# A hybrid recurrent decoder step on one core: ten convolution states moved as one contiguous tile instead of strided pieces per unit

## The chip, the core and the metric

The kernel runs on one NeuronCore of a Trainium2 chip. The core has a matrix engine (TensorE, PE in the profile, with its weight loads as PEld), three engines for elementwise work (VectorE or DVE, ScalarE or ACT, GpSimd or POOL), and SyncE (SP), which in this kernel issues every DMA. The engines run side by side, each in the order of its own instruction stream, and wait for each other by semaphores. The metric is device time in microseconds of the whole launch, as a median over runs. Inputs and outputs lie in HBM, tiles in SBUF, results of matmuls in PSUM.

## The reference, cut to what matters

One layer of a decoder is applied to 2048 prompt tokens and to 8 decode sequences of 4 tokens each. Its input projection is split among four head groups A to D; groups A and B put a short causal convolution over time on part of their channels:

```python
def _causal_conv(x, buf, w, b):
    t = x.shape[1]
    xx = jnp.concatenate([buf.astype(x.dtype), x], axis=1)
    y = b + xx[:, 0:t] * w[0]
    for j in range(1, CONV_K):
        y = y + xx[:, j:j + t] * w[j]
    return y, xx[:, t:]
...
    a_qkv, a_conv_new = _causal_conv(a_qkv, a_conv, conv_a_w, conv_a_b)
    aq, ak, av = _split(jax.nn.silu(a_qkv), (QK_A, QK_A, W_A))
    aq = _l2norm(heads(aq, H_A)) * DK_A ** -0.5
...
    b_xbc, b_conv_new = _causal_conv(b_xbc, b_conv, conv_b_w, conv_b_b)
```

`CONV_K` is 4, so the state of a channel is its last 3 inputs. Group A has 768 such channels and B has 512, together ten tiles of 128 channels. For the prompt the old state is zero; for each of the 8 decode sequences it is an input (3 x 8 numbers per channel), and the new states of both are outputs. After the convolution come the recurrences of the four groups ("mixing"), an output projection, a layer norm and a feed-forward layer.

## The kernel before

The prompt is cut into four blocks of 512 tokens (`NB`, `TB`). The 32 decode tokens ride along in the input projection of block 0, which so has 544 columns, and in the feed-forward layer of block 2. The work on TensorE is a sequence of weight units: `do_P` (L1870) goes through the 31 units of `PUNITS` for each block (one unit is 128 output channels of the input projection), `do_W` makes the output projection and `do_F` the feed-forward layer. `gemm` (L671) multiplies one unit: each weight tile comes by a DMA into `wraw`, is split by `w_split` (L642) into a rounded part `whi` (on ACT or DVE) and a rest `wlo` (on POOL or DVE), and three products are added up in PSUM. For 544 columns a unit takes two PSUM tiles of 272, and 48 matmuls.

What comes behind a unit is a generator that does one step and yields: `u_copy`, `u_gate`, `u_conv`, `u_cf` and `u_rows`. The first units of a block are one of rows and four copies; then come the six convolution units of group A, its two gates, the four convolution units of group B, and the others. A finished unit is stored to DRAM (`store_u`, L947, tensors UA to UD, and XA to XD for decode tokens). When all units of a group are stored, that group's chunks can start: `gen_A` (L1326) loads `laA` from UA, transposes it on TensorE, and so on; group A is one stream, the groups B, C and D are another.

All instructions of all engines are put down in one order by a planner that runs while the kernel is being built: `_Sim` keeps a clock for each engine and for the DMA queue, `_Run.tick` (L310) steps each generator once its clock says that its inputs are there. A `dma` (L472) counts in this, too: the end that `_Sim.move` works out for it becomes the time from which the generator may go on. Helpers such as `tvp` and `cpv` choose the engine of an instruction by those clocks. So whatever changes a clock may change the order and the engine of all that follows, but on the chip each engine then runs its stream strictly in order, and SP does so with its DMAs.

`u_conv` (L979) is the function at stake. `halo` is a small tile with the last three columns of the block before; POOL copies it to the front of `r`. In block 0 (`nt > TB`) a tile `rx` (named prx in the profile, 8 sequences x 7 columns, four buffers) takes the three old inputs of each sequence by a DMA (L988), and ACT evacuates the unit's PSUM into `r` and the last four columns of `rx`. After a yield the new states go out: in block 3 the prompt's, three columns of `r` (L1000), and in block 0 the decode sequences', three columns of `rx` (L1002). Then ACT makes the first tap for the prompt columns and, reading `rx`, for the decode columns; DVE adds three more taps for both; `sgm` (L935) makes the SiLU with DVE and ACT in turns. In the first four units of group A, ACT squares the result and TensorE sums it over each head with the constant `bones` (in the profile: pd<-g,con).

At the start, `ln0_start` (L776) loads the tokens, the first weights, the constants and the parameters in a written order, before anything else goes to SP.

Of the kernel before, what the change touches and what calls it, by code (L numbers as in the profile page):

```python
# [10 lines left out]
F32 = mybir.dt.float32  # L11
# [10 lines left out]
NB = 4  # L22
TB = 512
# [334 lines left out]
def _ap(x):  # L358
    return x[:] if callable(x.ap) else x
# [85 lines left out]
def kernel(ctx: ExitStack, tc: tile.TileContext, t):  # L445
# [3 lines left out]
    cst = ctx.enter_context(tc.tile_pool(name="cst", bufs=1))  # L449
# [17 lines left out]
    G = _Eng(R, "pool", nc.gpsimd, _pool_cost)  # L467
# [4 lines left out]
    def dma(out, in_, extra=0.0):  # L472
        nc.sync.dma_start(out=out, in_=in_)
        R.op("dma", R.sim.move(_ap(out), _ap(in_), extra))

    def A(out, in_, func, scale=1.0, bias=0.0):
        S.activation(out=out, in_=in_, func=func, scale=scale, bias=bias)
# [19 lines left out]
    def stt(out, a, s, b, op0, op1):  # L497
        V.scalar_tensor_tensor(out=out, in0=a, scalar=s, in1=b, op0=op0, op1=op1)
# [25 lines left out]
    def g2(dt=F32):  # L524
        return gp.tile([128, NTM], dt, tag="g", name="g")
# [31 lines left out]
    def PR(name, i=0, rows=128):  # L557
        return par[0:rows, PCOL[name] + i:PCOL[name] + i + 1]
# [14 lines left out]
    SD = cst.tile([128, 2, 2, 65], F32, name="SD")  # L573
    for z in (kzA, kzD, SA, SB, SC, SD):
        G.memset(z, 0.0)
    haloA = [cst.tile([128, 3], F32, name=f"haloA{i}") for i in range(6)]
    haloB = [cst.tile([128, 3], F32, name=f"haloB{i}") for i in range(4)]
    for z in haloA + haloB:
        G.memset(z, 0.0)

    epsT = cst.tile([128, 1], F32, name="epsT")
    G.memset(epsT, EPS)
# [43 lines left out]
    def w_get(i):  # L626
        w = sb4.tile([128, 4, 128], F32, tag="wraw", name="wraw")
        dma(w, units[i])
        raws[i] = w
# [146 lines left out]
    def ln0_start():  # L776
# [58 lines left out]
        for k in range(8):  # L835
            half, j = k // 4, k % 4
# [142 lines left out]
    def u_conv(b, ps, nt, g, j):  # L979
        w0 = "cAw" if g == "A" else "cBw"  # L980
        bn = "cAb" if g == "A" else "cBb"
        halo = (haloA if g == "A" else haloB)[j]
        cst_o, cst_s, cs_i = ("pa_conv", "sa_conv", "a_conv_in") if g == "A" else ("pb_conv", "sb_conv", "b_conv_in")
        r = g2()
        G.tensor_copy(r[:, 0:3], halo)
        if nt > TB:
            rx = sb4.tile([128, 8, 7], F32, tag="prx", name="prx")
            dma(rx[:, :, 0:3], t[cs_i][j * 128:j * 128 + 128])  # L988
        for p, a, e in segs(ps, nt):
            if a < TB:  # L990
                e1 = min(e, TB)
                cp(r[:, 3 + a:3 + e1], p[:, 0:e1 - a])
            if e > TB:
                a1 = max(a, TB)
                cp(rx[:, :, 3:7], p[:, a1 - a:e - a].rearrange("p (b t) -> p b t", b=8))
        z = g2()
        yield
        G.tensor_copy(halo, r[:, TB:TB + 3])
        if b == NB - 1:
            dma(t[cst_o][j * 128:j * 128 + 128], r[:, TB:TB + 3])  # L1000
        if nt > TB:
            dma(t[cst_s][j * 128:j * 128 + 128], rx[:, :, 4:7])  # L1002
        w = [PR(w0, j * 4 + k) for k in range(4)]
        A(z[:, 0:TB], r[:, 0:TB], AF.Identity, w[0], PR(bn, j))
        if nt > TB:
            zx = z[:, TB:nt].rearrange("p (b t) -> p b t", b=8)
            A(zx, rx[:, :, 0:4], AF.Identity, w[0], PR(bn, j))
        yield
        for k in range(1, 4):
            stt(z[:, 0:TB], r[:, k:k + TB], w[k], z[:, 0:TB], mult, add)  # L1010
            if nt > TB:
                stt(zx, rx[:, :, k:k + 4], w[k], zx, mult, add)
            yield
        for a in sgm(z, nt):
            yield
        tt(z[:, 0:nt], z[:, 0:nt], a[:, 0:nt], mult, tvp(nt, LATE_U))
        if g == "A" and j < 4:
            yield
            A(a[:, 0:nt], z[:, 0:nt], AF.Square)
            yield  # L1020
            pp = pieces(nt)
            for p, c0, cn in pp:
                mm(p[:, 0:cn], bones, a[:, c0:c0 + cn])
            for p, c0, cn in pp:
                ln(a[:, c0:c0 + cn], p[:, 0:cn], 1.0, epsT)
            ex(a[:, 0:nt], a[:, 0:nt], -0.5)
            yield
            stt(z[:, 0:nt], z[:, 0:nt], 0.125 if j < 2 else 1.0, a[:, 0:nt], mult, mult)
        R.hold(1.0)
        yield  # L1030
        store_u(b, g, j, z, nt)
# [1140 lines left out]

_OUT = {
    "y_prompt": (2048, D), "y_sample": (ND, D),
    "pa_conv": (768, 3), "pa_ssm": (128, 2, 2, 64), "pb_conv": (512, 3), "pb_ssm": (128, 2, 2, 64),
    "pc_ssm": (128, 2, 2, 64), "pd_mem": (128, 2, 2, 65), "pd_mstab": (4, 1),
    "sa_conv": (768, 8, 3), "sa_ssm": (128, 4, 4, 64), "sb_conv": (512, 8, 3), "sb_ssm": (128, 4, 4, 64),
    "sc_ssm": (128, 4, 4, 64), "sd_mem": (128, 4, 4, 65), "sd_mstab": (4, 8),
}
_KP = [0, 2, 1, 3]  # L2180
# [2 lines left out]
def _layout(i):  # L2183
    f = lambda x: np.ascontiguousarray(x, dtype=x.dtype)
    g = {k: np.asarray(v) for k, v in i.items()}
    a = {}
# [3 lines left out]
    z = np.zeros((D, 1), w.dtype)  # L2190
# [38 lines left out]
    m = np.zeros((16, 8), np.float32)  # L2229
    m[8:12] = g["state_d_mstab"][0].T  # L2230
    a["m_init"] = m
    a["a_conv_in"] = f(g["state_a_conv"][0].transpose(2, 0, 1))
    a["b_conv_in"] = f(g["state_b_conv"][0].transpose(2, 0, 1))

    def st(x):
        return f(x.reshape(4, 2, 4, 64, -1).transpose(1, 3, 0, 2, 4).reshape(128, 4, 4, -1))
# [8 lines left out]
def _unlayout(o):  # L2245
    def ps(x):
        y = np.stack([x[64 * h:64 * h + 64, :, h] for h in range(2)])
        return np.ascontiguousarray(y.transpose(2, 0, 1, 3).reshape(1, 1, 4, 64, -1))

    def ss(x):  # L2250
        return np.ascontiguousarray(x.reshape(2, 64, 4, 4, -1).transpose(2, 0, 3, 1, 4).reshape(1, 8, 4, 64, -1))

    inv = _KP
    pd, sd = ps(o["pd_mem"]), ss(o["sd_mem"])
    c = np.ascontiguousarray
    return (
        o["y_prompt"].reshape(1, 2048, D), o["y_sample"].reshape(8, 4, D),
        c(o["pa_conv"].T).reshape(1, 1, 3, 768), ps(o["pa_ssm"]), c(o["pb_conv"].T).reshape(1, 1, 3, 512), c(ps(o["pb_ssm"])[:, :, inv]),
        ps(o["pc_ssm"]), c(pd[..., 0:64]), c(pd[..., 64]), c(o["pd_mstab"].reshape(1, 1, 4)),
        c(o["sa_conv"].transpose(1, 2, 0))[None], ss(o["sa_ssm"]), c(o["sb_conv"].transpose(1, 2, 0))[None], c(ss(o["sb_ssm"])[:, :, inv]),  # L2260
        ss(o["sc_ssm"]), c(sd[..., 0:64]), c(sd[..., 64]), c(o["sd_mstab"].T)[None],
    )

# [17 lines left out]
```

## Time and profile before

| What | us |
|---|---|
| median of three runs | 3034.87 |
| the three runs | 3036.2, 3029.96, 3034.87 |
| profiled execution | 3030.68 |
| span of the profiled execution, first to last instruction | 3028.4 |
| TensorE busy, span | 2873.8 |
| VectorE busy | 2167.6 |
| GpSimd busy | 1592.5 |
| ScalarE busy | 1249.1 |
| mean granted clock of TensorE | 0.985 |

All times in the views are microseconds from the first instruction. L344 stands at nearly every compute instruction and L473 at nearly every DMA, since both go through helpers that record them; so instructions are told apart by their tiles: `g` are the general 128 x 544 tiles, `pd`, `pa__n` and `pb__n` PSUM tiles, `con` the constants, `par` the parameters, `a` and `b` tiles of the mixing streams. A row reads: output tiles <- input tiles, partitions x elements. DMA rows of SP show how long SP was held by issuing, not the landing. In the slices each digit is one fortieth of the span (75.7 us) in tenths; PEclk is the clock that was granted to TensorE, 1.00 being full speed.

### The profile page before, as it was taken

How to read it: one execution, taken by the hardware profiler on the slowest of the kernel's cores; microseconds unless marked ns; L12 is line 12 of the kernel's file. 1: busy time of each engine (PE TensorE's matmuls, PEld its weight loads, DVE VectorE, ACT ScalarE, POOL GpSimd, SP SyncE). 2: the span in 40 equal slices, each digit the busy share in tenths (PEclk: the TensorE clock that was granted, in tenths of full speed). 3: DMA queues.
4: the chain of work that ended last, by engine and by line, in shares of the span. 5: the costliest groups of instructions: out<-in, count | busy, mean ns of one | idle time of the engine just before them, and what ended most of it. 6: DMA issues, size and time to landing. Idle time of an engine off the chain costs nothing. (4 is left out here: it accounts for less than half of the span.)

```text
span 3028.4 us, 48058 instructions
## 1 busy us (share of the span) xinstructions
PE 2873.8 (95%) x16668; PEld 2472.5 (82%) x16668; DVE 2167.6 (72%) x4104; ACT 1249.1 (41%) x2658; POOL 1592.5 (53%) x1958
## 2 busy tenths in 40 slices
PE   7789989999999899999999999999999999999997
PEld 7779778777777778778777777778999999878886
DVE  7677887998897777778776867868664445484455
ACT  4554665574664533333334223333432222432222
POOL 4564845574756445644644465455354454454545
PEclk9899999999999999999999999999999999999999
DMA  5675546456566444445443444455333333333333
GB/s 170 99 183 168 161 132 209 143 159 195 154 174 199 127 124 135 129 132 157 144 141 95 128 133 133 127 149 165 108 105 91 86 117 91 108 114 98 98 95 100
DMA packets 361263, 407.11 MB, mean 134 GB/s; under 512 B 65468, under 2 KB 207804, under 8 KB 361020
## 3 DMA queue, kind: packets, MB, share of 16 engines
q1 hardware_dynamic: 361020, 404.04, 47.0%
q8 instruction: 132, 2.16, 0.3%
q14 instruction: 111, 0.91, 0.1%
HBM read 340.20 MB, written 63.72 MB: 133 GB/s over the span
## 5 line engine op out<-in xcount | busy, mean ns | idle before, releaser
L344 PE MATMUL pd<-g,whi 128*128 128x512 f32 (+2 forms) x8048 | 2224.4, 360 | 7.4 <-DVE g L344 5.5
L344 POOL TENSOR_TENSOR wlo<-wraw,whi 128x512 fp32r<-128x512 f32 x710 | 992.7, 1405 | 1218.5 <-ACT whi L344 1089.9
L344 PEld LDWEIGHTS pd<-g,whi 128*128 128x128 f32 x8048 | 1380.6, 189 | 206.6 <-DVE g L344 9.1
L344 PE MATMUL pd<-g,wlo 128*128 128x512 f32 (+2 forms) x4024 | 1297.7, 353 | 6.0 <-POOL wlo L344 3.7
L344 PEld LDWEIGHTS pd<-g,wlo 128*128 128x128 f32 x4024 | 715.2, 190 | 94.2 <-POOL wlo L344 6.1
L344 ACT ACTIVATE whi<-wraw 128x512 fp32r<-128x512 f32 x813 | 498.8, 626 | 363.0 <-PE pd L344 257.4
L344 DVE TENSOR_TENSOR g<-g 128x512 fp32r<-128x512 f32 (+5 forms) x364 | 357.2, 985 | 177.0 <-ACT g L344 163.5
L344 ACT ACTIVATE g<-pd 128x512 f32<-128x512 f32 (+1 forms) x329 | 167.6, 527 | 512.0 <-PE pd L344 510.5
L344 DVE TENSOR_TENSOR g<-g,pd 128x512 f32<-128x512 f32 (+2 forms) x288 | 159.5, 571 | 220.6 <-PE pd L344 219.9
L344 POOL TENSOR_TENSOR a<-nb,x 128x124 f32<-128x124 f32 (+30 forms) x496 | 199.0, 401 | 101.6 <-DMA nb<-ud32d 71.9
L344 ACT ACTIVATE g<-g 128x512 f32<-128x512 f32 (+5 forms) x334 | 206.5, 635 | 73.6 <-DVE g L344 65.6
L344 POOL TENSOR_TENSOR x<-x,a 128x124 f32<-128x124 f32 (+30 forms) x496 | 208.2, 420 | 38.9
L344 DVE CAST g<-g 128x512 fp32r<-128x512 f32 (+1 forms) x178 | 187.0, 1051 | 10.2 <-POOL g L344 3.2
L344 ACT ACTIVATE b<-b 128x256 f32<-128x256 f32 (+3 forms) x201 | 81.8, 408 | 214.7 <-DVE b L344 206.5
L344 DVE TENSOR_TENSOR wlo<-wraw,whi 128x512 fp32r<-128x512 f32 x122 | 95.9, 787 | 55.9 <-ACT whi L344 55.4
L344 DVE SCALAR_TENSOR_TENSOR g<-g,par 128x512 f32<-128x512 f32 (+1 forms) x128 | 119.3, 942 | 5.0 <-ACT g L344 5.0
L344 DVE TENSOR_TENSOR b<-laC 128x64 f32<-128x64 f32 (+2 forms) x467 | 115.6, 305 | 4.7 <-DMA laC<-UC 4.7
L344 DVE TENSOR_TENSOR kzD<-laC,b 64x128 f32<-64x128 f32 (+1 forms) x228 | 112.1, 492 | 1.7
L344 DVE SCALAR_TENSOR_TENSOR g<-g 128x512 f32<-128x512 f32 (+3 forms) x124 | 99.5, 805 | 18.9 <-ACT g L344 18.5
L344 DVE BATCH_NORM_STATS2 bst<-g 128x6 f32<-128x512 f32 (+1 forms) x98 | 65.9, 685 | 53.3 <-ACT g L344 48.5
L344 POOL TENSOR_TENSOR g<-g 128x512 f32<-128x512 f32 (+3 forms) x54 | 79.8, 1482 | 39.0 <-ACT g L344 39.0
L344 DVE TENSOR_SCALAR g<-g 128x512 int32<-128x512 int32 (+7 forms) x137 | 73.3, 549 | 20.3 <-ACT g L344 19.4
(2600 smaller groups left out, 2813.9 us busy)
## 6 DMA issues: line engine op xcount, KB each, us to landing
wraw<-in_w_dn_u_dram SPq DMA_DIRECT2D x264, 256.0 KB
wraw<-in_w_up_u_dram SPq DMA_DIRECT2D x256, 256.0 KB
wraw<-in_w_in_u_dram SPq DMA_DIRECT2D x248, 256.0 KB
nb<-ud32d SPq DMA_DIRECT2D x128, 256.0 KB
wraw<-in_w_out_u_dram SPq DMA_DIRECT2D x64, 256.0 KB
UC<-g SPq DMA_DIRECT2D x40, 256.0 KB
g<-in_x_prompt_dram SPq DMA_DIRECT2D x32, 256.0 KB
hTd<-g SPq DMA_DIRECT2D x32, 256.0 KB
```

The lines of the kernel that those rows point to most:

```text
L344: r = f(*a, **k)
```

## The change

The ten prompt halos become one tile `halos` of 128 x 10 x 3, cleared by one memset, and the decode states one tile `cvs` of 128 x 10 x 8 x 3. `cvs` is filled by one DMA in `ln0_start`, behind the first four weight tiles; its DRAM tensor has been laid out as the tile is, so that each partition's 240 numbers (960 bytes) lie in one piece on both sides. In `u_conv`, ACT copies a unit's 24 old inputs from `cvs` to `rx` in front of the evacuation, and after the yield copies the 24 new ones back to the same place. The last of the ten units stores the whole `cvs` in block 0, and the whole `halos` in block 3.

```diff
-    haloA = [cst.tile([128, 3], F32, name=f"haloA{i}") for i in range(6)]
-    haloB = [cst.tile([128, 3], F32, name=f"haloB{i}") for i in range(4)]
-    for z in haloA + haloB:
-        G.memset(z, 0.0)
+    halos = cst.tile([128, 10, 3], F32, name="halos")
+    cvs = cst.tile([128, 10, 8, 3], F32, name="cvs")
+    G.memset(halos, 0.0)
...
         w_get(1)
         w_get(3)
+        dma(cvs, t["conv_in"])
...
-        halo = (haloA if g == "A" else haloB)[j]
-        cst_o, cst_s, cs_i = ("pa_conv", "sa_conv", "a_conv_in") if g == "A" else ("pb_conv", "sb_conv", "b_conv_in")
+        halo = halos[:, j if g == "A" else 6 + j]
+        jj = j if g == "A" else 6 + j
         r = g2()
         G.tensor_copy(r[:, 0:3], halo)
         if nt > TB:
             rx = sb4.tile([128, 8, 7], F32, tag="prx", name="prx")
-            dma(rx[:, :, 0:3], t[cs_i][j * 128:j * 128 + 128])
+            cp(rx[:, :, 0:3], cvs[:, jj])
...
         G.tensor_copy(halo, r[:, TB:TB + 3])
-        if b == NB - 1:
-            dma(t[cst_o][j * 128:j * 128 + 128], r[:, TB:TB + 3])
+        if b == NB - 1 and jj == 9:
+            dma(t["p_conv"], halos)
         if nt > TB:
-            dma(t[cst_s][j * 128:j * 128 + 128], rx[:, :, 4:7])
+            cp(cvs[:, jj], rx[:, :, 4:7])
+            if jj == 9:
+                dma(t["s_conv"], cvs)
```

The outputs `p_conv` and `s_conv` are put back into the reference's shapes outside the launch. Three places show how the order moves. First ACT in block 0, around the third convolution unit of group A (its evacuation is the pair of rows before prx<-pd; g<-g of 128x544 are steps of `sgm` and squares of earlier units). Before:

```order
L344 ACTIVATE prx<-pd 128x8x4
L344 ACTIVATE whi<-wraw 128x512
L344 ACTIVATE g<-g 128x544
L344 ACTIVATE g<-g,par 128x512
L344 ACTIVATE g<-prx,par 128x32
L344 ACTIVATE g<-g 128x544 x2
L344 ACTIVATE whi<-wraw 128x512
L344 ACTIVATE g<-g 128x544
L344 ACTIVATE g<-pd,epsT 128x272 x2
```

Now:

```order
L344 ACTIVATE prx<-cvs 128x8x3
L344 ACTIVATE g<-pd 128x272
L344 ACTIVATE g<-pd 128x240
L344 ACTIVATE prx<-pd 128x8x4
L344 ACTIVATE whi<-wraw 128x512
L344 ACTIVATE g<-g 128x544
L344 ACTIVATE cvs<-prx 128x24
L344 ACTIVATE g<-g,par 128x512
L344 ACTIVATE g<-prx,par 128x32
L344 ACTIVATE g<-g 128x544 x2
L344 ACTIVATE whi<-wraw 128x512
L344 ACTIVATE g<-g 128x544
```

The rows are the same but for the two copies, prx<-cvs ahead of the evacuation and cvs<-prx ahead of the taps. Second, SP up to the first load of group A's first chunk, laA<-UA (wraw are weights, UA and XA stores of finished units of group A). Before:

```order
L473 DMA prx<-in_b_conv_in_dram 128x8x3
L473 DMA wraw<-in_w_in_u_dram 128x512
L473 DMA UA_161<-g 128x4x128
L473 DMA XA<-g 128x32
L473 DMA UA_161<-g 128x4x128
L473 DMA XA<-g 128x32
L473 DMA out_sb_conv_dram<-prx 1024x1x3
L473 DMA laA<-UA_161 128x768
```

Now:

```order
L473 DMA wraw<-in_w_in_u_dram 128x512 x2
L473 DMA UA_144<-g 128x4x128
L473 DMA XA<-g 128x32
L473 DMA UA_144<-g 128x4x128
L473 DMA XA<-g 128x32
L473 DMA laA<-UA_144 128x768
```

The strided load and store that stood between the stores of group A and laA are gone. Third, TensorE at the first use of laA (pa__n<-con,laA transposes it; pd<-g,whi and pd<-g,wlo are the weight products of block 0's units). Before:

```order
L344 MATMUL pd<-g,wlo 128x272 x2
L344 MATMUL pd<-g,whi 128x272 x2
L344 MATMUL pa__1954<-con,laA 128x128 x4
L344 MATMUL pd<-g,whi 128x272 x2
L344 MATMUL pd<-g,wlo 128x272 x2
L344 MATMUL pd<-g,whi 128x272 x2
L344 MATMUL pa__1987<-laA,kzA 128x128 x4
```

Now:

```order
L344 MATMUL pd<-g,wlo 128x272 x2
L344 MATMUL pd<-g,whi 128x272 x2
L344 MATMUL pa__1931<-con,laA 128x128 x4
L344 MATMUL pd<-g,whi 128x272 x2
L344 MATMUL pd<-g,wlo 128x272 x2
L344 MATMUL pd<-g,whi 128x272 x2
L344 MATMUL pd<-con,g 128x128 x4
L344 MATMUL pd<-g,whi 128x272 x2
L344 MATMUL pd<-g,wlo 128x272 x2
L344 MATMUL pd<-g,whi 128x272 x2
L344 MATMUL pa__1975<-laA,kzA 128x128 x4
```

Counted in weight products from the program's start, the transposes of laA stand at 786 now and stood at 774, the products of laA and kzA follow after 12 instead of 6, and the fourth of the norm matmuls pd<-g,con stands at 618 where it stood at 654. Further on the two orders differ throughout; TensorE has as many instructions as before. The chunks of group A stand between 63 weight products earlier and 63 later in the first six and 102 to 153 later from the seventh on.

More of the change, by code (lines that the diff above doesn't have):

```diff
@@ L2174 @@
     "y_prompt": (2048, D), "y_sample": (ND, D),
-    "pa_conv": (768, 3), "pa_ssm": (128, 2, 2, 64), "pb_conv": (512, 3), "pb_ssm": (128, 2, 2, 64),
+    "p_conv": (128, 10, 3), "pa_ssm": (128, 2, 2, 64), "pb_ssm": (128, 2, 2, 64),
     "pc_ssm": (128, 2, 2, 64), "pd_mem": (128, 2, 2, 65), "pd_mstab": (4, 1),
-    "sa_conv": (768, 8, 3), "sa_ssm": (128, 4, 4, 64), "sb_conv": (512, 8, 3), "sb_ssm": (128, 4, 4, 64),
+    "s_conv": (128, 10, 8, 3), "sa_ssm": (128, 4, 4, 64), "sb_ssm": (128, 4, 4, 64),
     "sc_ssm": (128, 4, 4, 64), "sd_mem": (128, 4, 4, 65), "sd_mstab": (4, 8),
@@ L2231, in _layout @@
     a["m_init"] = m
-    a["a_conv_in"] = f(g["state_a_conv"][0].transpose(2, 0, 1))
-    a["b_conv_in"] = f(g["state_b_conv"][0].transpose(2, 0, 1))
+    cv = np.concatenate([g["state_a_conv"][0].transpose(2, 0, 1), g["state_b_conv"][0].transpose(2, 0, 1)], 0)
+    a["conv_in"] = f(cv.reshape(10, 128, 8, 3).transpose(1, 0, 2, 3))
     def st(x):
@@ L2254, in _unlayout @@
     pd, sd = ps(o["pd_mem"]), ss(o["sd_mem"])
+    pc = o["p_conv"].transpose(1, 0, 2).reshape(1280, 3)
+    sc = o["s_conv"].transpose(1, 0, 2, 3).reshape(1280, 8, 3)
     c = np.ascontiguousarray
@@ L2257, in _unlayout @@
         o["y_prompt"].reshape(1, 2048, D), o["y_sample"].reshape(8, 4, D),
-        c(o["pa_conv"].T).reshape(1, 1, 3, 768), ps(o["pa_ssm"]), c(o["pb_conv"].T).reshape(1, 1, 3, 512), c(ps(o["pb_ssm"])[:, :, inv]),
+        c(pc[:768].T).reshape(1, 1, 3, 768), ps(o["pa_ssm"]), c(pc[768:].T).reshape(1, 1, 3, 512), c(ps(o["pb_ssm"])[:, :, inv]),
         ps(o["pc_ssm"]), c(pd[..., 0:64]), c(pd[..., 64]), c(o["pd_mstab"].reshape(1, 1, 4)),
-        c(o["sa_conv"].transpose(1, 2, 0))[None], ss(o["sa_ssm"]), c(o["sb_conv"].transpose(1, 2, 0))[None], c(ss(o["sb_ssm"])[:, :, inv]),
+        c(sc[:768].transpose(1, 2, 0))[None], ss(o["sa_ssm"]), c(sc[768:].transpose(1, 2, 0))[None], c(ss(o["sb_ssm"])[:, :, inv]),
         ss(o["sc_ssm"]), c(sd[..., 0:64]), c(sd[..., 64]), c(o["sd_mstab"].T)[None],
```

## The prediction

> **What bounds the kernel now.** I read the page first (busy times and slices), then the granted clock and busy time by stretch, then the waits of the stretch that stood out, and last the time line of that stretch, engine by engine. From the page, the busy line and the slices of TensorE and of its clock:
>
> ```profile
> PE 2873.8 (95%) x16668; PEld 2472.5 (82%) x16668; DVE 2167.6 (72%) x4104; ACT 1249.1 (41%) x2658; POOL 1592.5 (53%) x1958
> ...
> PE   7789989999999899999999999999999999999997
> ...
> PEclk9899999999999999999999999999999999999999
> ```
>
> TensorE is busy 95% of the span, so whatever gains must come out of its idle 5%, or out of a low clock. Both are at the front: slices 2 and 3 (76 to 227 us). The busy time by stretch, whose columns are length, then busy time of PE, PEld, DVE, ACT and POOL, granted clock, DMA share and GB/s:
>
> ```profile
> 60.00:200.00 140.00, 109.28 (x794) 106.65 (x793) 100.43 (x186) 78.70 (x186) 69.13 (x64) 0.88 0.62 119
> 200.00:2200.00 2000.00, 1912.99 (x10503) 1589.86 (x10503) 1595.43 (x3284) 900.14 (x1978) 1088.63 (x1551) 0.99 0.51 148
> 2200.00:3028.00 828.00, 808.09 (x5070) 734.35 (x5068) 427.63 (x562) 244.83 (x447) 407.62 (x297) 0.99 0.35 101
> ```
>
> From 60 to 200 us TensorE idles 30.7 of 140 us, at a clock of 0.88; the next 2000 us hold 87.0 us of idle time at 0.99, the rest 19.9 us. 60 to 200 us is where the ten convolution units of block 0 run, the only ones with decode tokens and with the strided transfers. The waits of 55 to 200 us (engine, what it waited for: us in total, times, longest):
>
> ```profile
> POOL wlo L344 <- ACT whi L344: 54.6, 18, 9.2
> ACT g L344 <- DMA prx<-in_a_conv_in_dram: 20.6, 4, 9.1
> ...
> PE pd L344 <- ACT g L344: 16.8, 2, 9.4
> ACT g L344 <- DMA prx<-in_b_conv_in_dram: 15.4, 2, 9.9
> DVE g L344 <- ACT g L344: 14.2, 5, 9.8
> ...
> PE pa__1954 L344 <- DMA laA<-UA: 12.2, 1, 12.2
> ```
>
> ACT stands still 36.0 us for the strided loads; PE, DVE and POOL then stand for ACT. TensorE has three long gaps, here from its time line (start, duration, and in brackets the idle time before it and who ended it):
>
> ```profile
> 90.82 2.18 PE L344 MATMUL pd<-g,con 128*128 128x272 f32 x4 [9.43 <-ACT g L344]
> ...
> 123.69 2.18 PE L344 MATMUL pd<-g,con 128*128 128x272 f32 x4 [7.34 <-ACT g L344]
> ...
> 165.20 1.12 PE L344 MATMUL pa__1954<-con,laA 128*128 128x128 f32 x4 [12.15 <-DMA laA<-UA]
> ```
>
> 28.9 of the 30.7 us are these three. Each is followed by matmuls at half clock:
>
> ```profile
> 40.00:45.00 5.00, 5.00 (x42) 5.00 (x42) 2.27 (x4) 3.86 (x9) 2.58 (x2) 1.00 0.96 296
> ...
> 80.00:85.00 5.00, 1.39 (x12) 1.17 (x10) 0.00 (x0) 0.00 (x0) 1.13 (x1) 1.00 0.74 98
> 85.00:90.00 5.00, 0.00 (x0) 0.00 (x0) 0.27 (x1) 1.92 (x4) 0.00 (x0) 0.54 0.93 128
> 90.00:95.00 5.00, 4.18 (x14) 3.71 (x15) 4.96 (x10) 3.18 (x8) 3.32 (x4) 0.50 0.31 67
> 95.00:100.00 5.00, 5.00 (x37) 4.92 (x36) 3.48 (x9) 2.98 (x9) 4.17 (x4) 0.93 0.12 10
> ...
> 120.00:125.00 5.00, 1.31 (x3) 1.08 (x4) 4.62 (x8) 3.57 (x9) 3.10 (x3) 0.50 0.67 139
> 125.00:130.00 5.00, 5.00 (x22) 4.77 (x22) 5.00 (x10) 4.49 (x9) 3.76 (x3) 0.52 0.31 107
> ...
> 165.00:170.00 5.00, 4.80 (x22) 4.80 (x23) 0.92 (x3) 1.03 (x4) 0.00 (x0) 0.50 1.08 214
> ```
>
> Read the last columns too: at 40 us the DMA engines move 296 GB/s at a share of 0.96; at 85 us, among strided packets, 128 GB/s at 0.93. So those transfers also hold up what shares the queue.
>
> **The change, part by part.** The profiled execution took 3030.68 us, its span 3028.4; the sum goes against 3030.68, which lies 4.2 us under the median and inside the three runs.
>
> *First gap.* ACT's rows around it, POOL's multiply that the next unit step needs, and the SP row of the load that ACT waits for:
>
> ```profile
> 76.86 0.20 ACT L344 ACTIVATE prx<-pd 128x32 f32<-128x32 f32 x1
> ...
> 78.19 0.80 ACT L344 ACTIVATE g<-g,par 128x512 f32<-128x512 f32 x1
> 88.05 0.41 ACT L344 ACTIVATE g<-prx,par 128x32 f32<-128x32 f32 x1 [9.06 <-DMA prx<-in_a_conv_in_dram]
> ...
> 90.13 0.64 ACT L344 ACTIVATE g<-g 128x544 f32<-128x544 f32 x1
> ```
> ```profile
> 79.49 1.64 POOL L344 TENSOR_TENSOR g<-g 128x544 f32<-128x544 f32 x1
> ```
> ```profile
> 75.14 0.60 SPq L473 DMA_DIRECT2D prx<-in_a_conv_in_dram  x1
> ```
>
> The load is issued at 75.14 and used at 88.05, 12.9 us later. Behind it in ACT's order stands the square (90.13) of an earlier unit, for which PE's norm matmul waits. Its input is ready when POOL ends, at 81.13. With the states already in SBUF the square ends at about 81.8, against 81.39 when PE runs dry: the gap falls from 9.43 to 0.4. **-9.0 us**.
>
> *Second gap.* The same at the last unit of group A:
>
> ```profile
> 111.17 0.85 ACT L344 ACTIVATE g<-g,par 128x512 f32<-128x512 f32 x1
> 119.41 0.41 ACT L344 ACTIVATE g<-prx,par 128x32 f32<-128x32 f32 x1 [7.39 <-DMA prx<-in_a_conv_in_dram]
> ```
>
> ACT's wait of 7.39 is the whole of PE's 7.34. **-7.3 us**.
>
> *Third gap.* PE waits for the first load of group A's chunk, which can't be issued before the group's last store has landed (SP's rows); the nearest load of that kind without strided neighbours is laC much later, SP's issue and PE's use:
>
> ```profile
> 153.40 0.95 SPq L473 DMA_DIRECT2D UA<-g  x1
> ...
> 156.41 0.33 SPq L473 DMA_DIRECT2D laA<-UA  x1
> ```
> ```profile
> 1229.48 0.33 SPq L473 DMA_DIRECT2D laC<-UC  x1
> ```
> ```profile
> 1236.06 0.41 PE L344 MATMUL pb__13863<-con,laC 128*128 128x128 f32 x2 [1.28 <-DMA laC<-UC]
> ```
>
> From issue to use it is 8.8 us for laA (384 KB) and 6.6 us for laC (512 KB). A faster landing alone is worth 2.2 us; the rest depends on how early the last store goes out, and that hangs behind ACT's waits of 7.39 us and behind SP, which issues all of it in order. Ends: nothing, or the 12.15 whole. I take two thirds, since both causes shrink: **-8 us**.
>
> *Clock.* The loss of the three slow stretches is busy time by missing clock: 4.18 x 0.50 + 5 x 0.07 = 2.4; 1.31 x 0.50 + 5 x 0.48 = 3.1; 4.80 x 0.50 = 2.4. The first gap begins at 81.39 and the clock is still 1.00 up to 85, so a rest of under 3.6 us leaves it alone: **-8 us** (0 if the gaps stay long). [...]
>
> *Added on ACT.* Twenty small copies; the nearest rows, of the tile prx (minimum/median/maximum ns):
>
> ```profile
> L473 SPq DMA_DIRECT2D prx<-in_a_conv_in_dram x6: 587/600/1312, 59.7 to 107.6; - x6
> L344 ACT ACTIVATE prx<-pd x6: 198/205/224, 63.2 to 177.3; 128x32 f32<-128x32 f32 x6
> L473 SPq DMA_DIRECT2D out_sa_conv_dram<-prx x6: 555/614/3165, 63.5 to 110.3; - x6
> ```
>
> 20 x 0.205 = 4.1 us on an engine with 78.7 busy of 140: it lies beside other work except where DVE waits for ACT. Ends 0 and +4.1; **+1 us**. No new wait stands before a PSUM read: the copy in front reads a tile that landed 50 us before; the copy behind waits only for ACT's own work, and the one store at the end holds nothing but SP.
>
> *DVE.* It has 100.43 us of work in these 140. If the stage shrinks by 32, that is 93% of 108: now DVE is what comes late next. Ends 0 and +16.3 (the first two terms whole, if PE's norm matmuls end up waiting for DVE instead). In the first gap itself DVE stands still (0.00 and 0.27 us in the stretches from 80 and 85 us), so I stay near the low end: **+4 us**.
>
> *SP and the start.* 30 issues go, 3 come. Twenty of those that go are at 0.6 us each, some 12 us of SP, while SP waits anyway: 0. The new load stands behind four weight loads and ahead of the first hTx store; a load of the same kind:
>
> ```profile
> 9.01 0.33 SPq L473 DMA_DIRECT2D par<-in_params_dram  x1
> ```
>
> 0.33 us of issue and 120 KB, at 296 GB/s 0.4 us, done before any hTx store is ready: 0, at most +0.8. The fewer memsets and the ten small stores of block 3 lie off TensorE's path: 0, at best -3 for the stores.
>
> *The order of the rest.* The planner lets a unit's next step wait for the end of each transfer, so with thirty fewer its clocks move and the whole order is laid anew. TensorE's work is equal; the idle 87.0 us of 200 to 2200 us may move either way. A tenth is 9 us: 0, ends -9 and +9.
>
> Sum: -9.0 - 7.3 - 8 - 8 + 1 + 4 = -27.3; 3030.68 - 27.3 = **3003 us**.
>
> [...]
>
> **The rivals.** *The third gap stays* because the last store of group A or its load is late for other reasons (DVE's chain of the gate, the load's 6.6 us): only the first two gaps and their clock go, -9.0 - 7.3 - 5.5 + 1 + 4 = -16.8, 3014 us. For it: laC's landing; against it: ACT idles in the very stretch before. *DVE takes ACT's place*: the norm matmuls wait for DVE, terms one and two come back with their clock, the third stays won: -8 - 2.4 + 1 + 4 = -5.4, 3025 us, about no change. For it: DVE is busy 4.96 and 5.00 of 5 us in the stretches from 90 and 125 us; against it: 0.00 and 0.27 in those from 80 and 85 us, in the gap itself, where it waits for ACT. *The new order is worse*, the other side: in 200 to 2200 us group A's chunks stand some 130 weight matmuls later from the seventh chunk on, and each chunk's chain of small matmuls may meet inputs later than planned. The price is idle time on top of 87.0 us. It decides from 27 us (then no change), and is slower by over 0.2% from 33 us, that is from 120 us of idle; at 130 it would be 3046 us. Against it: TensorE's instructions are the same in number, and that would be a rise by half. That the change doesn't do what it says can be left out: the order of the built program has one load and two stores where the thirty transfers were.
>
> **How the numbers follow.** Forecast 0.68, third gap stays 0.14, DVE 0.11, worse order 0.07. The forecast's own range is 2990 to 3016. Downward the ends add the rest of the third gap and the good end of the order, -27.3 - 4 - 9 - 3 = 2987; upward the range takes in the third-gap case with the order's bad end, 3014 + 9 = 3023. Within 0.2% (6 us, what a measurement of this kernel can tell) is 3025 to 3037: part of the DVE case and a little of the worse order, 0.08. Slower 0.06, faster 0.86.
>
> **What would show it.** Right: no ACT wait on prx, no gap over 4 us on PE between 60 and 200 us, clock 0.95 or more there, the end of block 0's units some 27 us earlier, idle time from then to the end of mixing near 87 us. Wrong: PE's norm matmuls waiting for DVE; an idle time after 200 us that is 30 us larger; a gap before laA as long as now.

## The result, and the profile after

The changed kernel takes 2996.51 us (median of 4 runs, 2995.88 to 2997.66) beside 3034.05 us of the kernel before (4 runs): ratio 0.9874, 95% interval 0.9857 to 0.9892, faster by 37.5 us. The forecast was 3003 (2987 to 3023), faster at 0.86. The profiled execution took 2997.66 us, 33.0 less than the profiled one of before. The page of after, busy line, slices, clock and packets:

```profile
PE 2871.2 (96%) x16668; PEld 2470.2 (82%) x16668; DVE 2178.9 (73%) x4096; ACT 1248.7 (42%) x2683; POOL 1603.4 (54%) x1953
...
PE   7899999999999999999999999999999999999997
...
PEclk9999999999999999999999999999999999999999
...
DMA packets 339454, 407.10 MB, mean 136 GB/s; under 512 B 43404, under 2 KB 185996, under 8 KB 339212
```

The low slices at the front are gone. The same three stretches as before (length, busy PE, PEld, DVE, ACT, POOL, clock, DMA share, GB/s):

```profile
60.00:200.00 140.00, 127.46 (x956) 125.15 (x955) 118.45 (x211) 96.68 (x239) 82.04 (x85) 0.95 0.50 150
200.00:2200.00 2000.00, 1923.91 (x10603) 1601.16 (x10602) 1610.19 (x3286) 898.07 (x1981) 1097.89 (x1543) 0.99 0.50 147
2200.00:2996.00 796.00, 775.93 (x4802) 701.82 (x4800) 405.17 (x528) 228.57 (x417) 395.38 (x287) 0.99 0.35 102
```

TensorE idles 12.5 us in the first where it idled 30.7, and the clock is 0.95 for 0.88. But from 200 to 2200 us the idle time fell too, from 87.0 to 76.1. The waits of 55 to 200 us hold no line on prx, cvs or laA any more:

```profile
POOL wlo L344 <- ACT whi L344: 46.1, 18, 6.7
ACT g L344 <- PE pd L344: 17.3, 11, 4.2
DVE g L344 <- ACT g L344: 11.6, 6, 8.7
...
ACT whi L344 <- DMA wraw<-in_w_in_u_dram: 9.5, 2, 9.2
...
PE pd L344 <- ACT g L344: 7.6, 3, 3.3
```

TensorE's time line at the places of the three gaps (the transposes of laA start without a wait), and two more gaps near 3 us:

```profile
83.41 1.45 PE L344 MATMUL pd<-g,con 128*128 128x272 f32 x4 [2.78 <-ACT g L344]
...
113.72 1.18 PE L344 MATMUL pd<-g,con 128*128 128x272 f32 x4 [1.55 <-ACT g L344]
...
125.52 0.60 PE L344 MATMUL pd<-g,whi 128*128 128x272 f32 x1 [3.28 <-ACT g L344]
...
141.62 0.60 PE L344 MATMUL pa__1931<-con,laA 128*128 128x128 f32 x4
...
193.80 0.82 PE L344 MATMUL pd<-g,whi 128*128 128x272 f32 x2 [2.98 <-ACT whi L344]
```

The first matmul of 512 columns, where block 1 begins, starts at 254.39 us; before it was 277.43.

**How the runs below are read.** A kernel's work in 60 to 200 us is taken as PE's busy time there less half of what was busy while the granted clock was 0.50. Half is an estimate: in the kernel before the 272-column products start 0.23 us apart from 127.03 to 129.52 us, at 0.50, and 0.13 us apart from 129.91 to 130.41 us, at 1.00. (Busy time times the mean clock of the row would not do: in the kernel before, 17.6 of the 34.1 us at half clock lie in the gaps themselves, where nothing is lost.) The stretches at half clock, before, then after:

```profile
85.45:95.69 10.24, 4.87 (x17) 4.40 (x18) 5.78 (x11) 5.79 (x13) 4.01 (x4) 0.50 0.56 80
119.58:129.82 10.24, 6.13 (x23) 5.67 (x24) 9.44 (x17) 8.33 (x18) 6.68 (x5) 0.50 0.56 123
157.13:170.78 13.65, 5.58 (x26) 5.58 (x27) 2.82 (x9) 2.59 (x6) 2.58 (x5) 0.50 0.80 133
```
```profile
84.19:87.61 3.42, 3.42 (x16) 3.28 (x15) 3.39 (x9) 3.16 (x10) 2.04 (x3) 0.50 0.28 78
125.16:128.57 3.41, 3.05 (x13) 3.05 (x14) 0.66 (x3) 3.41 (x11) 1.71 (x2) 0.50 0.41 93
193.42:200.00 6.58, 5.67 (x23) 5.35 (x24) 3.87 (x5) 6.16 (x15) 4.11 (x4) 0.50 0.76 215
```

So the clock costs 8.3 us before and 6.1 after. Work before is 109.28 - 8.3 = 101.0, after 127.46 - 6.1 = 121.4, a gain of 20.4 us in this stretch. What a kernel's median gains against before, less that, came from elsewhere: 37.5 - 20.4 = 17.1 for the change. The stretch is read from one profiled execution and the gain from medians, and executions of one kernel can lie 10 us and more apart (25 of the kernel before took 3023.64 to 3041.34 us), so a few us in such a difference mean little.

### The profile page after: what moved, and what is told of

Read it like the earlier page. It is cut to its first block, busy times and chain, and to the rows that moved or that the text cites. A ratio compares the mean times of both kernels' runs of the same rounds, so it can differ in the third digit from the quotient of the medians.

```text
span 2996.0 us, 48004 instructions
## 1 busy us (share of the span) xinstructions
PE 2871.2 (96%) x16668; PEld 2470.2 (82%) x16668; DVE 2178.9 (73%) x4096; ACT 1248.7 (42%) x2683; POOL 1603.4 (54%) x1953
## 4 chain that ended last, share of the span: by engine, by line
PE 63%; DVE 20%; POOL 5%; issue 4%; ACT 3%; DMA 3%; SPq 1%; DVEq 0%; POOLq 0%; ACTq 0%
PE pd L344 53%; DVE g L344 10%; DVE b L344 5%; ACT g L344 2%; POOL wlo L344 2%; DVE kzD L344 2%; DVE a L344 1%; SPq L473 1%; POOL x L344 1%; DMA nb<-ud32d 1%; POOL g L344 1%; POOL a L344 1%; DMA wraw<-in_w_in_u_dram 1%; DVE wlo L344 1%; DMA laC<-UC 1%
## 5 line engine op out<-in xcount | busy, mean ns | idle before, releaser
L344 PEld LDWEIGHTS pd<-g,wlo 128*128 128x128 f32 x4024 | 716.4, 190 | 98.1 <-POOL wlo L344 11.5
L344 DVE TENSOR_TENSOR g<-g 128x512 fp32r<-128x512 f32 (+5 forms) x359 | 366.7, 1024 | 183.6 <-ACT g L344 170.2
L344 POOL TENSOR_TENSOR a<-nb,x 128x124 f32<-128x124 f32 (+30 forms) x496 | 201.7, 407 | 81.8 <-DMA nb<-ud32d 51.8
L344 ACT ACTIVATE g<-g 128x512 f32<-128x512 f32 (+4 forms) x337 | 207.3, 634 | 64.4 <-DVE g L344 56.9
L344 DVE CAST g<-g 128x512 fp32r<-128x512 f32 (+1 forms) x175 | 177.7, 1016 | 6.4 <-POOL g L344 0.9
L344 DVE TENSOR_TENSOR b<-laC 128x64 f32<-128x64 f32 (+2 forms) x471 | 125.9, 325 | 5.9 <-DMA laC<-UC 5.9
L344 DVE SCALAR_TENSOR_TENSOR g<-g 128x512 f32<-128x512 f32 (+3 forms) x124 | 112.4, 910 | 9.9 <-ACT g L344 9.2
L344 POOL TENSOR_TENSOR g<-g 128x512 f32<-128x512 f32 (+3 forms) x59 | 86.4, 1469 | 38.5 <-ACT g L344 27.5
```

The source lines that it names most:

```text
L344: r = f(*a, **k)
```

## The experiments

The change does two things at once: it alters the transfers, and since the planner sees other transfers, it lays a new order on all engines. The kernels e1 to e5 and e11 to e14 set these apart. In them a call that starts with plan_ tells the planner of an operation that isn't issued, and raw_cp or nc.sync.dma_start issues one that it isn't told of; so each has one kernel's order, instruction for instruction on PE, DVE and POOL, with the other's transfers. All times are medians, each beside runs of before made along with it (median 3037.69 for e1 to e4, 3034.37 for e5, e8, e11 and e12, 3034.80 for e7, e9, e13 and e14).

### The new transfers in the old order (e1_old_order)

```diff
+        nc.sync.dma_start(out=cvs, in_=t["conv_in"])
...
-            dma(rx[:, :, 0:3], t[cs_i][j * 128:j * 128 + 128])
+            raw_cp(rx[:, :, 0:3], cvs[:, jj])
+            plan_dma(rx[:, :, 0:3], t["conv_in"][:, jj])
...
-            dma(t[cst_s][j * 128:j * 128 + 128], rx[:, :, 4:7])
+            raw_cp(cvs[:, jj], rx[:, :, 4:7])
+            plan_dma(t["s_conv"][:, jj], rx[:, :, 4:7])
+            if jj == 9:
+                nc.sync.dma_start(out=t["s_conv"], in_=cvs)
```

> All transfers are the changed ones, but the planner is told of the old ones, so that the order of every engine is the old one. Theory 1, the transfers themselves cost the time in the stage of the convolution units: 3034 less the 23 us by which that stage got shorter, 3011 us, give or take 4, without the three long gaps of TensorE. Rival, the newly laid order did it: 3028 or more.

Measured: 3004.36 us, ratio 0.9900 (0.9881 to 0.9919). Its row of 60 to 200 us:

```profile
60.00:200.00 140.00, 129.63 (x986) 126.67 (x985) 127.62 (x224) 100.30 (x246) 92.49 (x95) 0.98 0.54 157
```

129.63 us busy, 3.4 of them lost to the clock: 126.2 us of work, 25.2 more than before. The transfers alone bring nearly what the sum gave to the stage (27.3), and the time is 6.6 us below the 3011 that I expected. Of its 33.3 us 8.1 come from elsewhere.

### The strided transfers in the new order (e2_new_order_strided)

```diff
-        dma(cvs, t["conv_in"])
+        plan_dma(cvs, t["conv_in"])
...
-            cp(rx[:, :, 0:3], cvs[:, jj])
+            nc.sync.dma_start(out=rx[:, :, 0:3], in_=t["conv_in"][:, jj])
+            plan_cp(rx[:, :, 0:3], cvs[:, jj])
```

and in the same way for the stores.

> The strided transfers per unit, in the order that the planner lays for the changed kernel. Theory 1: most of the gain goes, what stays is the 9 us that the rest of the order gave: about 3024 us, with waits of ACT for prx as long as in the kernel before. Rival, the order did it: 3005 or less.

Measured: 3009.36 us, ratio 0.9919 (0.9899 to 0.9939): 28.3 us of gain with the thirty strided transfers still there. Its work in the stretch is 124.66 - 6.9 = 117.8 us, and ACT waits 15.3 us for prx where it waited 36.0. That went against my theory. But this kernel's strided transfers run from and to the changed kernel's DRAM arrays (128 x 10 x 8 x 3), and a unit's states are no longer one run of 12 KB there. So it mixes three things: order, number of transfers and layout in DRAM. The next two are mixed in the same way, and the later ones take it apart.

### One half at a time (e3_load_only, e4_store_only)

Before's order; in e3 the one early load and strided stores, in e4 strided loads and the one late store, the strided ones in the new DRAM layout.

> Old order; the states are loaded once at the start, while the ten strided stores per unit (and the ten small ones of block 3) stay. If ACT's waits for the loads are what counts: nearly all of what the old order with all new transfers gains, 3013 us. If the strided stores clog the queue that the weights come through: less than half of it, 3022 or more, with waits for weights in place of those for prx.

> Old order; the ten strided loads per unit stay, the new states go out by one contiguous store. If the loads count: ACT still waits for them, though they find the queue emptier; 3026 us, a gain of 8. If the stores clog the queue: the loads land quickly, ACT's waits on prx fall under 10 us in all, and the time is 3014 or less.

Measured: e3 3010.57 us, ratio 0.9917 (0.9898 to 0.9935); e4 3006.78 us, ratio 0.9912 (0.9892 to 0.9933). Either half alone seems enough for most of the gain, which no sum of separate terms allows.

### The layout in DRAM alone (e11_layout_only)

```diff
-            dma(rx[:, :, 0:3], t[cs_i][j * 128:j * 128 + 128])
+            dma(rx[:, :, 0:3], t["conv_in"][:, jj])
...
-            dma(t[cst_s][j * 128:j * 128 + 128], rx[:, :, 4:7])
+            dma(t["s_conv"][:, jj], rx[:, :, 4:7])
```

> Before's order and its strided transfers at each unit, thirty of them as before; only the arrays in DRAM are laid out as in the changed kernel (128 x 10 x 8 x 3, so that a unit's states are no longer one run of 12 KB). The three runs that keep strided transfers (3006.8, 3009.4, 3010.6) all had this layout, so they leave open whether it or the order and the single transfers brought them down. If the layout does it (it changes the form of the transfer: SP issued these loads in 0.43 us, before in 0.60): 3009 +- 5. If it is the order and the number of strided transfers, as I held so far: 3034 +- 4, the same as before, with ACT waiting about 36 us for prx between 55 and 200 us. My own theory has changed with the traces: I expect 3009, with ACT waiting 15 us or less.

Measured: 3018.87 us, ratio 0.9953 (0.9933 to 0.9973). Some 60% of the gain that I expected, but clearly not nothing: thirty transfers as before, in before's order, cost 15.5 us less because their DRAM side is laid out in another way. Its waits of 55 to 200 us and the tile prx on SP (minimum/median/maximum ns):

```profile
ACT g L344 <- DMA prx<-in_conv_in_dram: 18.5, 5, 10.0
...
PE pa__1946 L344 <- DMA laA<-UA: 7.3, 1, 7.3
```
```profile
L473 SPq DMA_DIRECT2D prx<-in_conv_in_dram x10: 384/433/496, 59.0 to 150.6; - x10
L473 SPq DMA_DIRECT2D out_s_conv_dram<-prx x10: 388/394/759, 62.8 to 160.4; - x10
```

A transfer of as many pieces now issues in 0.43 and 0.39 us, against 0.60 and 0.61, and none is held up for long (0.76 at most, before 3.2). Work in the stretch is 124.64 - 5.8 = 118.8 us, 17.8 more than before.

### The new order with the old transfers (e12_new_order_old_dram)

As e2, with the loads and stores on before's DRAM arrays: the changed kernel's order and nothing else of the change.

> The changed kernel's order on every engine, with the strided transfers per unit and the DRAM arrays of before (no copies on ACT). If the layout in DRAM is what counts: 3026 +- 6, ACT waits about 30 us for prx, and gaps of 7 us or more are back on PE between 60 and 200 us. If the new order alone avoids the waits: 3009 +- 4 like the earlier run with strided transfers in the new order. I expect 3026.

Measured: 3019.49 us, ratio 0.9949 (0.9929 to 0.9970).

```profile
60.00:200.00 140.00, 115.66 (x830) 112.64 (x829) 104.56 (x192) 84.08 (x197) 66.67 (x69) 0.90 0.64 118
```
```profile
ACT g L344 <- DMA prx<-in_a_conv_in_dram: 16.4, 4, 8.8
ACT g L344 <- DMA prx<-in_b_conv_in_dram: 13.9, 3, 10.2
```

ACT's waits are back (30.3 us), PE's gaps with them (9.7 and 5.4 us), and the stretch gains 4.7 us only (115.66 - 9.9 = 105.7 of work): there is no wait for laA, which stands later in this order. The other 10.2 of the 14.9 come behind the stretch. So the stage is decided mainly by the transfers; the order spares it the third gap and adds something later. The time lies between what the two cases gave.

### 96-byte pieces at the unit (e5_unit_contig)

Against e1, whose one load and one store go:

```diff
+            nc.sync.dma_start(out=cvs[:, jj], in_=t["conv_in"][:, jj])
             raw_cp(rx[:, :, 0:3], cvs[:, jj])
...
+            nc.sync.dma_start(out=t["s_conv"][:, jj], in_=cvs[:, jj])
```

> Before's order; each unit loads its own states and stores them when before did, but into the contiguous tile, in 128 pieces of 96 bytes in place of 1024 of 12, with the copies on ACT. If the number of pieces is what costs: 3004 +- 4, like the run with the two single transfers in the old order, and no ACT wait for the states over 3 us. If it is the place in the queue, behind weight loads of 256 KB: ACT still waits 3 to 8 us at three or four units, 3012 to 3025. I expect 3006, between 3002 and 3012.

Measured: 3010.33 us, ratio 0.9921 (0.9898 to 0.9943).

```profile
60.00:200.00 140.00, 125.37 (x957) 122.90 (x956) 120.50 (x215) 96.14 (x238) 84.34 (x90) 0.98 0.53 152
```
```profile
ACT prx L480 <- DMA cvs<-in_conv_in_dram: 22.1, 6, 7.3
```

The time came out between the two cases, the wait as in the second: with an eighth of the pieces ACT still waits 22.1 us for its loads, which are issued behind weight loads, and TensorE loses only 4.2 us of work by it against e1 (125.37 - 3.4 = 122.0). ACT's waiting time was a poor measure of TensorE's loss.

### The clean halves (e13_load_only_old_store, e14_store_only_old_load)

e13 is e3 with the strided stores on before's DRAM arrays, e14 is e4 with the strided loads from before's.

> Half of the change, cleanly: before's order, the states come by the one early load and a copy, while the stores stay strided per unit and go to before's DRAM arrays. No ACT wait for the states is possible, so the first two gaps go. If the loads are what costs: first block done 24 us earlier or more, 3009 +- 5. If the old form of the stores also holds the queue: PE's wait for laA stays at 7 to 12 us and the weight loads behind them come late, first block 15 to 20 us earlier, 3017 +- 5. I expect 3013.

> The other half: before's order, strided loads per unit out of before's DRAM arrays, the states going out through the contiguous tile by one store. If the loads are late because of their own form and the weight loads ahead of them: ACT still waits 25 us or more for prx, the first two gaps stay, only the wait for laA goes: 3022 +- 5. If they are late because of the stores in the same queue: ACT waits under 10 us, 3009 +- 5. I expect 3018, with the third load landing about 8 us after its issue (10.6 in before, 7.5 in the new layout).

Measured: e13 3020.06 us, ratio 0.9953 (0.9937 to 0.9968); e14 3008.89 us, ratio 0.9920 (0.9904 to 0.9936). For both I had expected a time between the two cases; each came out at the end that blames the stores. The stretch of e13 and its wait for laA, then the stretch of e14 and its wait for prx:

```profile
60.00:200.00 140.00, 121.27 (x933) 118.33 (x932) 116.11 (x207) 93.01 (x220) 86.95 (x84) 0.96 0.73 147
```
```profile
PE pa__1947 L344 <- DMA laA<-UA: 10.7, 1, 10.7
```
```profile
60.00:200.00 140.00, 130.51 (x987) 127.96 (x986) 126.11 (x223) 98.56 (x235) 89.17 (x93) 0.96 0.57 156
```
```profile
ACT g L344 <- DMA prx<-in_b_conv_in_dram: 4.0, 1, 4.0
```

This settles that the stores cost, and how the halves hang together. With the old stores gone, the old strided loads cause 4.0 us of waiting on ACT in place of 36.0, and the stretch gains 24.4 us (130.51 - 5.1 = 125.4 of work): the loads were late because of the stores in the same queue. With the loads gone and the old stores left, the stretch gains 18.9 (121.27 - 1.4 = 119.9): the first two gaps go, since no load is left to wait for, and TensorE still waits 10.7 us for laA. So the first two gaps need both, a load at the unit and the stores that make it late; the third needs the stores alone. Two pairs show what it is about the stores. e13 and e3 differ only in the array that the stores run into; e3 waits 5.6 us for laA in place of 10.7, and gains 27.1 us in place of 14.7 (its interval, 0.9898 to 0.9935, lies just below that of e13). e14 and e4 differ only in the array that the loads come from, and their intervals overlap.

From 66 to 72 us, behind the first unit's store and with a weight load and a strided load issued, first before, then e14 (no strided store) and e11 (stores in the new layout):

```profile
66.00:72.00 6.00, 6.00 (x51) 6.00 (x50) 6.00 (x18) 3.41 (x8) 1.58 (x3) 1.00 0.13 23
```
```profile
66.00:72.00 6.00, 6.00 (x51) 5.99 (x50) 5.93 (x21) 3.21 (x8) 0.74 (x2) 1.00 0.41 101
```
```profile
66.00:72.00 6.00, 6.00 (x50) 5.99 (x50) 6.00 (x19) 4.09 (x9) 1.59 (x3) 1.00 0.39 101
```

The queue moves 23 GB/s in before, at a share of 0.13, and 101 in the others: its engines are not busy with small pieces in these 6 us, they mostly stand still. But the queue stands in the others, too. In e11 it moves nothing for 2 us behind the first store, earlier than in before, and next to nothing for 3 us behind the second; and in e14 it moves nothing for 2 us with a weight load and a strided load issued and no strided store ahead of them:

```profile
65.00:67.00 2.00, 2.00 (x18) 2.00 (x18) 2.00 (x2) 0.00 (x0) 1.81 (x2) 1.00 0.00 0
73.00:76.00 3.00, 3.00 (x26) 3.00 (x25) 3.00 (x6) 2.76 (x9) 1.53 (x1) 1.00 0.01 1
```
```profile
75.00:77.00 2.00, 2.00 (x18) 2.00 (x17) 2.00 (x3) 1.65 (x5) 1.65 (x1) 1.00 0.00 0
```

So the stores in the old layout prolong something that also happens without them. The third unit's load shows the consequence: SP's row of it and ACT's use in e14, to be held against 75.14 and 88.05 in before.

```profile
74.02 0.59 SPq L473 DMA_DIRECT2D prx<-in_a_conv_in_dram  x1
```
```profile
79.27 0.42 ACT L344 ACTIVATE g<-prx,par 128x32 f32<-128x32 f32 x1
```

Used 5.3 us after issue, without a wait; in before it was 12.9. The stores of e13 and of e3 are both of 12-byte pieces, and yet the wait for laA is 10.7 us in one and 5.6 in the other; so by these runs the size of the pieces alone isn't the cause. What in the old layout makes the queue stand longer wasn't tried further and stays open.

### The order laid anew (e7_after_land165, e8_after_land155, e9_before_land165)

One constant of the planner, the time that it allows for a transfer to land, is 1.60 in both kernels.

```diff
-    LAND = 1.6
+    LAND = 1.65
```

(1.55 in e8; e7 and e8 are the changed kernel, e9 is before.) No work changes, only the order.

> The changed kernel with one constant of the planner moved from 1.60 to 1.55 us (the time it allows for a transfer to land), which lays the order anew everywhere and changes no work. If the order after the first block is worth only a few us by itself: 2997 +- 4. If what separates the changed kernel from the run with its transfers in the old order (7.8 us) is a lucky order: 3000 to 3012. I expect 2999, between 2993 and 3008.

> The changed kernel with the planner's landing time moved from 1.60 to 1.65 us: no work is changed, the order is laid anew. If the changed kernel's order happens to be a good one, this falls near the run with 1.55 (3009): 3004 to 3012. If not, 2997 +- 4. I expect 3006. The first block should be done at 252 +- 5 us as in both others.

> The kernel before with the planner's landing time moved from 1.60 to 1.65 us, all transfers as before. If laying the order anew is worth up to 10 us to either side by itself: 3024 to 3044. If before's order was an unlucky one: 3020 +- 5. I expect 3031, with the wait of ACT for prx still over 20 us.

Measured: e8 3008.67 us, ratio 0.9907 (0.9883 to 0.9931); e7 3024.79 us, ratio 0.9968 (0.9957 to 0.9980); e9 3032.98 us, ratio 0.9993 (0.9980 to 1.0006), no difference that shows. The first stretches of e8 and e7 hold as much work as the changed kernel's 121.4:

```profile
60.00:200.00 140.00, 127.93 (x960) 125.70 (x959) 118.99 (x210) 97.57 (x241) 83.14 (x85) 0.95 0.51 152
```
```profile
60.00:200.00 140.00, 127.92 (x962) 125.50 (x962) 120.16 (x225) 99.44 (x244) 84.34 (x97) 0.96 0.53 155
```

127.93 - 6.2 = 121.7 and 127.92 - 5.6 = 122.3 (though in e7 block 1 begins at 260.3 us, not near the 252 that I expected). So e8 is slower than I expected by some 10 us and e7 by 19, and both for the order alone. What separates these kernels from the changed one lies behind, above all in 1050 to 1550 us; after, then e7:

```profile
1050.00:1550.00 500.00, 488.02 (x2619) 404.88 (x2618) 396.99 (x845) 177.77 (x428) 255.76 (x415) 1.00 0.49 142
```
```profile
1050.00:1550.00 500.00, 474.00 (x2522) 394.48 (x2520) 381.78 (x829) 175.69 (x421) 248.57 (x396) 0.97 0.46 135
```

With the half-clock time taken off as above, 486.3 us of work against 462.8: 23.5 us in one stretch (the profiled execution of e7 took 3032.83 us, the slowest of its 12 runs, so some of it is chance). So the order of the rest is worth that much between neighbouring settings, with identical work.

### The runs side by side

Work in 60 to 200 us against before's 101.0, the median's gain, and what is left for all other stretches (us):

| run | order | loads, stores | 60 to 200 | gain | rest |
|---|---|---|---|---|---|
| e12 | new | old, old | +4.7 | 14.9 | +10.2 |
| e2 | new | strided, new layout, both | +16.8 | 28.3 | +11.5 |
| after | new | one, one | +20.4 | 37.5 | +17.1 |
| e11 | old | strided, new layout, both | +17.8 | 15.5 | -2.3 |
| e13 | old | one, old | +18.9 | 14.7 | -4.2 |
| e14 | old | old, one | +24.4 | 25.9 | +1.5 |
| e5 | old | 96-byte pieces, both | +21.0 | 24.0 | +3.0 |
| e3 | old | one, new layout | +23.4 | 27.1 | +3.7 |
| e4 | old | new layout, one | +23.8 | 30.9 | +7.1 |
| e1 | old | one, one | +25.2 | 33.3 | +8.1 |
| e8 | LAND 1.55 | one, one | +20.7 | 25.7 | +5.0 |
| e7 | LAND 1.65 | one, one | +21.3 | 10.0 | -11.3 |
| e9 | before with LAND 1.65 | old, old | +2.4 | 1.8 | -0.6 |

The three kernels in the changed order have 10.2 to 17.1 in the last column, the seven in the old order -4.2 to +8.1. In the stage the terms don't add: in the old order one load for the old ones gives 18.9, one store 24.4, both together 25.2. No kernel tried was faster than the changed one.

## Why the prediction was right, and where its steps were not

The sign and the place were right: the stage of the ten units in block 0 gave 20.4 us, beside 27.3 in the sum. All the signs it named came but two: the 512-column matmuls start 23.0 us earlier, not 27, and the idle time of 200 to 2200 us is 11 us less, not the same. That the total lies only 6.5 us below the forecast is partly luck, since two terms were mis-sized in opposite ways: the clock gave far less than its 8 us, and the order of the rest, priced at 0, gave more than the stage fell short. In the profiled pair: idle time in 60 to 200 us 18.2 less, beside 19.3 in the sum; clock 2.2 less (8.3 lost against 6.1), beside 8; the rest 12.6, beside 0; together 33.0.

- *First gap, -9.0 forecast: 9.43 became 2.78, -6.7.* The step that failed is that the square ends at 81.8, as soon as POOL has multiplied. ACT's rows in the changed kernel:

```profile
80.95 1.34 ACT L344 ACTIVATE g<-g 128x544 f32<-128x544 f32 x2 [1.59 <-DVE g L344]
82.20 0.61 ACT L344 ACTIVATE whi<-wraw 128x512 fp32r<-128x512 f32 x1
82.72 0.64 ACT L344 ACTIVATE g<-g 128x544 f32<-128x544 f32 x1
```

Two more operations and a weight split stand ahead of the square, and the first waits 1.59 us for DVE. They stood there before as well, in the "..." of the rows that the prediction quotes, between 88.05 and 90.13.

- *Second gap, -7.3: 7.34 went, and 1.55 stands ahead of the norm matmuls that follow, -5.8.* ACT's rows of the same kind end it. Three gaps are new: 3.28 for ACT, 1.33 for DVE, and 2.98 at 193.80, where ACT has waited 9.2 us for weights. The last comes with the new order: e2 has one of 2.36 there, e1 none.
- *Third gap, -8: went whole, -12.15.* Two thirds was the wrong choice between the ends, and laC's 6.6 us the wrong row to choose by: in e14 laA is used without a wait 3.7 us after its issue (135.43 and 139.10). Nor are ACT's waits ahead of the last store what makes the gap: e13 has none for the states, yet laA goes out 7.0 us after the last store to UA and is used 5.8 us later. What counted was the strided stores: in the old order the wait is gone where the states leave by one store (e1, e4, e14) or by ten of 96-byte pieces (e5), and is 5.6, 7.3 and 10.7 where they leave by ten strided ones (e3, e11, e13). In the new order it is gone in e2 and e12 too, with strided stores.
- *Clock, -8: -2.2.* This is the step that failed most. The loss before was read rightly (7.9 in the sum, 8.3 by the rows above), but "a rest of under 3.6 us leaves it alone" does not hold: the gaps of 2.78, 3.28 and 2.98 us each go with a stretch at 0.50 (from 84.19, 125.16 and 193.42 us), and 6.1 us stay lost (last section).
- *ACT's copies and DVE, +1 and +4.* The copies take 0.22 to 0.23 us each. DVE ends one gap, of 1.33 us; the rival in which the norm matmuls wait for DVE did not come. But ACT waits for DVE ahead of the gaps of 2.78, 1.55 and 3.28 us (1.59, 2.34 and 2.02 us), so DVE does come late next, by way of ACT. The three new gaps are 7.6 us, for the 5 of these two terms.
- *SP and the start, 0.* The weight matmul behind the first 384 starts 0.76 us earlier (74.45 for 75.21), so the early load costs nothing there.
- *Order of the rest, 0, ends -9 and +9: -12.6 in the profiled pair, -17.1 by the medians.* A tenth of the idle time was too narrow. Not all of it is the order: e1, with the same transfers in the old order, gains 8.1 us outside the stage, and what those are isn't shown. By the medians, the kernels with the same transfers in other orders range there from 11.3 us lost (e7) to 17.1 won. The rival "the new order is worse" had the right mechanism, and e7 shows a part of its size: had the planner's constant been 1.65 in both kernels, the change would have brought 8 us (3032.98 to 3024.79).

The cause that the prediction gave for the lost time is half refuted. ACT did stand still for strided loads and TensorE for ACT; but these loads were late because of the strided stores ahead of them (36.0 us of waits with them, 4.0 in e14 without), and the more so as those ran into an array in which a unit's states are one run (18.5 us in e11, where they are not). The sum has no term for the stores but SP's issue time, at 0. And the parts of the change can't be priced one by one: the one load alone brings the first two gaps down to 1.6 us or less (e13), the one store alone all three to 3.0 or less (e14).

## What to carry to other kernels

When a load lands late, look at what was issued ahead of it in its queue before pricing the load: a moved or merged store can be worth more than the load for which an engine visibly waits (here the one store alone gained 25.9 us, e14, and the one load alone 14.7, e13). Separate a change of work from the order that a planner makes of it, by running each with the other's; where a small change of a planner's constant moves the time as much as the edit under test, a single comparison says little about the edit, and the last few us of a gain are chance. Price a slow clock only over the time in which the engine works, and don't take short gaps for free: here they kept most of the clock's loss (6.1 of 8.3 us). An experiment that undoes one part should keep the rest to the byte: here the new array shape, carried along in three of them, was worth 15.5 us by itself and blurred what they showed.

## What was not expected of the hardware

- Stores of 1024 pieces of 12 bytes held up what was issued behind them for longer where the pieces ran into one 12 KB run than where they went into an array with a stride of 960 bytes; the number of pieces is the same (before and e2, which differ in this layout too, both have 65468 packets under 512 B). TensorE's wait for laA is 10.7 us with the first (e13) and 5.6 with the second (e3), with equal loads. Behind the first unit's store the queue moves 23 GB/s at a share of 0.13 from 66 to 72 us in before, and 101 GB/s in e11.
- The clock fell after shorter rests than the prediction's 3.6 us, and the length of a rest did not decide alone. In the traces of before and after the granted clock changes only at marks that lie 3.41 us apart: the stretches of 10.24 and 13.65 us at 0.50 in the rows of the result above are three and four times as long. Here are a gap of 2.94 us in e1 and one of 1.92 us in e8, each with the stretches between the marks around it:

```profile
82.67 1.18 PE L344 MATMUL pd<-g,con 128*128 128x272 f32 x4 [2.94 <-ACT g L344]
```
```profile
78.12:81.53 3.41, 1.61 (x13) 1.39 (x12) 2.02 (x3) 1.78 (x5) 1.76 (x2) 1.00 0.79 279
81.53:84.94 3.41, 2.27 (x14) 2.11 (x15) 3.35 (x5) 2.56 (x6) 2.25 (x3) 1.00 0.13 21
84.94:88.36 3.42, 3.42 (x30) 3.42 (x29) 3.38 (x6) 3.36 (x12) 2.84 (x3) 1.00 0.45 135
```
```profile
81.88 1.19 PE L344 MATMUL pd<-g,con 128*128 128x272 f32 x4 [1.92 <-ACT g L344]
```
```profile
79.52:82.93 3.41, 1.49 (x9) 1.11 (x8) 2.82 (x4) 2.56 (x5) 1.57 (x2) 1.00 0.25 93
82.93:86.34 3.41, 3.41 (x17) 3.41 (x16) 3.38 (x8) 3.38 (x11) 2.29 (x3) 0.50 0.38 101
```

The mark at 81.53 splits the longer gap into 1.80 and 1.14 us of idle time, and the clock stays at 1.00. The shorter one lies whole between two marks, 1.92 us idle of 3.41, and the next stretch runs at 0.50. In the traces of before and after, from 28 to 2950 us, the least idle time between two marks that took the clock from 1.00 to 0.50 is 1.45 us (after, 411.87 to 415.29 us), and the most that left it at 1.00 is 1.91 (before, 682.78 to 686.19 us):

```profile
411.87:415.29 3.41, 1.96 (x20) 1.72 (x20) 3.41 (x7) 1.11 (x2) 3.31 (x3) 1.00 0.72 215
415.29:418.70 3.41, 3.41 (x15) 3.03 (x14) 2.24 (x7) 1.16 (x3) 0.00 (x0) 0.50 0.65 210
```
```profile
682.78:686.19 3.41, 1.50 (x7) 0.90 (x5) 3.41 (x10) 3.08 (x7) 1.82 (x5) 1.00 0.65 202
686.19:689.61 3.41, 2.75 (x20) 2.60 (x21) 3.41 (x7) 1.02 (x3) 2.03 (x4) 1.00 0.57 154
```

So the idle time between two marks doesn't settle it alone either; what else does isn't shown here.
